# Moving matmul operands to fixed offsets within 256 bytes of an SBUF partition

## The chip, the core and the metric

The kernel runs on one core of a Trainium2 chip. The metric is the device time of one execution in microseconds (us). The engines have these names in the profile: PE is TensorE's matmul, PEld its weight load, DVE is VectorE, ACT is ScalarE, POOL is GpSimd, SP is SyncE, which here issues DMAs.

## The reference

256 tokens of 1024 features, float32, pass through five layers in a row. Each one normalises, multiplies by weight matrices and adds its result to the residual `x`.

```
x = x + mixer(rmsnorm(x))            # gated delta rule and mLSTM over w_in (1024 x 5648), then w_out
x = x + w2(silu(w1 h) * w3 h)        # hidden size 2816
x = rmsnorm(x + gate(h) * ple)       # per-layer embedding
x = x + gate * rglru(h);  x = x + gate * peer_ffn(h)     # peer: 16384 experts, u and v of 1024 each
x = x + gate * fox_attention(h);  x = x + gate * peer_ffn(h)
```

In `peer_ffn` every token picks 128 of 16384 experts. The kernel computes all experts with dense matmuls and weights them by a matrix that holds zeros for the experts not picked.

## The kernel before, in words

**Split precision.** Every large product is taken in three terms. A float32 weight tile of 128 x 1024 arrives by DMA as `raw`. ACT writes its rounded copy `whi` (type float32r, line 209), and DVE or POOL writes the rest, `wlo = raw - whi` (lines 257 and 259). The activations have the same two parts, in tiles with an h and an l: `hh`/`hl` for the normalised input, `fh`/`fl` in the feed-forward layer, `oab` in the mixer, `xbh`/`xbl` in the recurrent layer, `p0`/`p1` for the embedding, and `rawh`/`rawl` for the input before its norm is known. The matmuls are high times high, high times low and low times high.

**Stream.** The class `Stream` hands out one weight tile after another in a fixed order, 766 in all, with four buffers of `raw` and two each of `whi` and `wlo`. SP's queue issues the loads. The order of all instructions is a planner's, at build time.

**Three loops use them.** `block` (matmul at line 323) makes one output of 128 features x 256 tokens from one weight tile: 24 matmuls, in which a 128 x 128 piece of the weights is loaded into the array and 256 columns of the activations are streamed through. `kblock` (line 1051) is the same with one activation tile and eight outputs. `tblock` (line 1065) turns it round: a 128 x 128 piece of `hh` or `hl` is loaded, and 512 columns of `whi` or `wlo` are streamed, 12 matmuls for one weight tile. Inputs of a norm with a shift are streamed with 258 columns.

**Stages by time.** Mixer to about 290 us; feed-forward to about 460 (22 hidden tiles, three weight tiles each); embedding and recurrent layer to about 660; first peer layer: queries and selection to 811, `u` (128 blocks of line 323) to 1126, `v` (120 of line 1065 and 8 of line 1051) to about 1480; attention to about 1660; second peer layer likewise, `u` from 1822 to 2136 and `v` from there to the end. During `u`, DVE also builds one-hot matrices (lines 1584 to 1591), from which small float16 matmuls (line 1600) make the weighting.

**Where the tiles stand.** Tiles follow each other in a partition by their sizes, behind 16384 bytes of DMA scratch and 128 of constants. So before the change `hh` starts 24704 bytes into each partition and `hl` 32896, both 128 bytes beyond a multiple of 256. The stream's buffers start at 44480 and all stand 192 beyond one. `oab`, `xbh`, `xbl`, `p0`, `p1` and the 256-wide `rawh` and `rawl` also stand 192 beyond, `fh` and `fl` 0. Every slice that a matmul takes of them is a multiple of 256 bytes long, so all slices of a tile stand alike. The 258-wide `rawh` and `rawl` are the exception: each of their eight rows is 1032 bytes long, and so stands 8 bytes further on than the row before it.

Of the kernel before, what the change touches and what calls it, by code (L numbers as in the profile page):

```python
# [8 lines left out]
F32 = mybir.dt.float32  # L9
FR = mybir.dt.float32r  # L10
# [7 lines left out]
P = 128  # L18
S = 256
D = 1024  # L20
KC = D // P
NFF = 22
NR = 11
EPS = 1e-6
BIG = 1e30
TB = 8
TAIL = 8
NLATE = 3
# [11 lines left out]
def _constants():  # L40
# [6 lines left out]
    z[C_IOTA] = c + 0 * r  # L47
    z[C_NGT] = np.where(c > r, -BIG, 0.0)
    z[C_NLT] = np.where(c < r, -BIG, 0.0)
    for i, b in enumerate(LBS):  # L50
# [131 lines left out]
class Stream:  # L182
# [16 lines left out]
    def _ahead(self, b, n, loads, his, los):  # L199
        while self.nl < min(n, loads) or self.nh < min(n, his) or self.ns < min(n, los):  # L200
            if self.nl < min(n, loads) and self.nl < self.ns + b.raw_bufs:
                t = b.spool.tile([P, D], F32, name="raw", tag="raw", bufs=b.raw_bufs)[:, :self.width(self.nl)]
                self.load = b.nc.sync.dma_start(t, self.seq[self.nl])
                self.raw[self.nl] = t
                self.nl += 1
                continue
            if self.nh < min(n, his) and self.nh < self.nl:
                t = b.spool.tile([P, D], FR, name="whi", tag="whi", bufs=b.hi_bufs)[:, :self.width(self.nh)]
                b.nc.scalar.copy(t, self.raw[self.nh])  # L209
                self.hi[self.nh] = t  # L210
                self.nh += 1
                continue
            if self.ns < self.nh:
                i = self.ns
                t = b.spool.tile([P, D], FR, name="wlo", tag="wlo", bufs=b.lo_bufs)[:, :self.width(i)]
                b.sub(t, self.raw.pop(i), self.hi[i].bitcast(F32), i)
                self.lo[i] = t
                self.ns += 1
                continue
            raise AssertionError  # L220
# [9 lines left out]
class Build:  # L230
# [29 lines left out]

    def mark(self, label):
        pass

    def ahead_of(self, gen, prio):

# [86 lines left out]
    def setup(self):  # L352
        nc, pp, d = self.nc, self.pp, self.d
        self.xT = pp.tile([P, KC, S], F32, name="xT")
        self.hh = pp.tile([P, KC, S], FR, name="hh")
        self.hl = pp.tile([P, KC, S], FR, name="hl")
        with self.tc.high_priority(offset=5000):
            for k in range(0, KC, 2):
                nc.sync.dma_start(self.xT[:, k:k + 2], d["xT"][:, k:k + 2])
        self.cst = pp.tile([P, N_PERSIST, P], F32, name="cst")  # L360
        self.cols = pp.tile([P, N_COLS], F32, name="cols")
        nc.scalar.dma_start(self.cols, d["cols"])
        nc.scalar.dma_start(self.cst, d["const"][:, :N_PERSIST])
        self.ident = self.cst[:, C_ID]
        self.ones = self.cst[:, C_ONE]
        self.mhalf = pp.tile([P, 1], F32, name="mhalf")
        nc.vector.memset(self.mhalf, -0.5)
        self.lam = self.colr("lam")
        self.mods = [pp.tile([P, 24], F32, name=f"mod{i}") for i in range(4)]
        self.gsc = [pp.tile([P, KC], F32, name=f"gsc{i}") for i in range(4)]  # L370

        order = []

        def add(k, lo=0, hi=None):
            n = d[k].shape[0]
            order.extend(d[k][i] for i in range(lo, n if hi is None else hi))

        add("w_in")
        add("w_ba")
        add("w_bb")  # L380
        add("w_out")
        for j in range(NFF):
            add("w1", j, j + 1)
            add("w3", j, j + 1)
            if j:
                add("w2", j - 1, j)
        add("w2", NFF - 1, NFF)
        add("w_ple")
        add("w_pg")
        for j in range(NR + GLAG):  # L390
            if j < NR:
                add("l_in", j, j + 1)
            if j >= GLAG:
                i = j - GLAG
                order.append(d["l_gate"][i][:, :2 * len(PAIRS[i]) * P])
        add("l_in", NR, 2 * NR)
        add("l_out")
        for l in (0, 1):
            if l:
                add("f_in")  # L400
                add("f_out")
            add(f"q{l}")
            add(f"u{l}")
            add(f"v{l}")
        self.ws = Stream(self, order)
# [83 lines left out]
                                            op0=OP.mult, op1=OP.subtract)  # L489

    def raw_tiles(self, pool, wide=True):
        w = S + 2 if wide else S
        return (pool.tile([P, KC, w], FR, name="rawh"), pool.tile([P, KC, w], FR, name="rawl"),
                pool.tile([P, S], F32, name="rawb"),
                lambda: (pool.tile([P, S], F32, name="rawt", bufs=2), pool.tile([P, 1], F32, name="rawc", bufs=2)))

# [78 lines left out]
    def mix(self, mp, scr):  # L575
        nc = self.nc
# [1 line left out]
        gab = mp.tile([P, 16, S], F32, name="gab")  # L578
        gz = mp.tile([P, H, S], F32, name="gz")
        mo = mp.tile([P, H, S], F32, name="mo")  # L580
        oab = mp.tile([P, 16, S], FR, name="oab")
        self.oab = [oab[:, 4 * i:4 * i + 4] for i in range(4)]
        self.norm(scr, self.colr("g_mix"), raw=(
            oab[:, 0:8], oab[:, 8:16], gab[:, 0], lambda: (gab[:, 1 + self.nraw % 2], None)))
# [57 lines left out]
        for src, o in ((self.oa, 0), (self.ob, 8)):  # L642
            for b in range(4):
                wh, wl = self.ws.get()
                for n in range(2):
# [7 lines left out]
                    else:  # L653
                        t = mp.tile([P, S], F32, name="mixt", bufs=2)
# [417 lines left out]
    def ffn(self, fp, scr, fin):  # L1072
        nc = self.nc
        self.sub_pattern = "D"
        self.phase("ffn")
        self.norm(scr, self.colr("g_ffn"), raw=self.raw_tiles(fp, False), paced=True)
        self.bg.append(self.mod_task)
        accs = [self.acc() for _ in range(4)]
        hm = {}
        for j in range(NFF + 1):  # L1080
            if j < NFF:
                p1 = self.linear(self.mmt())
                p3 = self.linear(self.aux("p3"))
                s = fp.tile([P, S], F32, name="fs", bufs=2)
                nc.scalar.activation(s, p1, AF.Silu)
                nc.vector.tensor_tensor(s, s, p3, op=OP.mult)
                h = fp.tile([P, S], FR, name="fh", bufs=3)
                l = fp.tile([P, S], FR, name="fl", bufs=3)
                self.split(h, l, s)
                hm[j] = (h, l)  # L1090
            if j:
                self.kblock(accs, *hm.pop(j - 1), j == 1, j == NFF)
            self.tick()
            if j == 8:
                pT = fin.tile([P, 2, S], F32, name="pT")
                nc.scalar.dma_start(pT, self.d["pT"])
                self.p_split = [fin.tile([P, 2, S], FR, name=f"p{i}") for i in range(2)]
                for k in range(2):
                    self.split(self.p_split[0][:, k], self.p_split[1][:, k], pT[:, k])
        for n in range(KC):  # L1100
            nc.vector.tensor_tensor(self.xT[:, n], self.xT[:, n], accs[n // 2][:, (n % 2) * S:(n % 2 + 1) * S],
                                    op=OP.add)
# [74 lines left out]
    def lru(self, fin, scr):  # L1177
        nc = self.nc
        with ExitStack() as es:
            lp = es.enter_context(self.tc.tile_pool(name="lru", bufs=1))  # L1180
            xb = lp.tile([P, NR, S], F32, name="xb")
            xh = lp.tile([P, NR, S], FR, name="xbh")
            xl = lp.tile([P, NR, S], FR, name="xbl")
            hs = lp.tile([P, NR, S], F32, name="hs")
            lam = self.lam
            self.phase("lru")
# [60 lines left out]
    def fox(self):  # L1247
# [3 lines left out]
        with ExitStack() as es:  # L1251
# [68 lines left out]
            def scores(h):  # L1320
# [5 lines left out]
                for i, (a, b, k) in enumerate(((0, P, mask[:, P:]), (P, 384, mask))):  # L1326
                    nc.vector.tensor_tensor_reduce(out=L[:, a:b], in0=ps[:, a:b], in1=k, scale=1.0, scalar=-BIG,
                                                   op0=OP.add, op1=OP.max, accum_out=m[:, i:i + 1])
# [95 lines left out]
    def peer(self, l):  # L1424
        nc = self.nc
# [3 lines left out]
        with ExitStack() as es:  # L1429
            gp = es.enter_context(self.tc.tile_pool(name="peer", bufs=1))  # L1430
            big = gp.tile([P, P, S], F32, name="big")
            flat = big.rearrange("p a b -> p (a b)")

            def region(kb, size):
# [3 lines left out]
            es1 = es.enter_context(ExitStack())  # L1438
            rp = es1.enter_context(self.tc.tile_pool(name="raw", bufs=1))
            self.phase(f"peer{l}")  # L1440
            self.norm(big[:, 112:128], self.gsc[mi], self.mods[mi][:, 0:8], raw=(
                rp.tile([P, KC, S + 2], FR, name="rawh"), rp.tile([P, KC, S + 2], FR, name="rawl"), big[:, 0],
                lambda: (big[:, 1 + self.nraw % 2], flat[:, 3 * S + self.nraw:3 * S + self.nraw + 1])))
            qT = region(0, 4096).rearrange("p (a b) -> p a b", a=16)
            sk = region(16, 2048).rearrange("p (a b) -> p a b", a=16)
# [125 lines left out]
            def spread():  # L1571


                nonlocal held
                H = TB // 2
                iop = io[:, None].to_broadcast([P, H, P, 2])
# [3 lines left out]

                for t0 in range(0, S, TB):
                    tq = slice(t0, t0 + TB)
# [36 lines left out]
            for a in range(16):  # L1619
# [5 lines left out]
                if a % 4 == 3:  # L1625
                    for tb in range(2):
                        ps = self.aux("sc")
                        for i in range(4):
                            b = a - 3 + i
# [10 lines left out]
            for e in range(P):  # L1640
# [4 lines left out]
                if held:  # L1645
                    a = op.tile([P, S], F32, name="act", bufs=3)
# [46 lines left out]
            for e in range(P):  # L1693
# [6 lines left out]
                h, l_ = self.hh[:, e % 4], self.hl[:, e % 4]  # L1700
# [40 lines left out]
```

## Time and profile before

| what | value |
|---|---|
| time, median of 3 runs | 2492.12 us (2492.01 to 2500.49) |
| the profiled execution's own time | 2497.24 us |
| its span, first to last instruction | 2495.4 us |
| PE busy, of the span | 95% |
| DVE, ACT, POOL busy | 77%, 50%, 29% |
| matmuls, each with a weight load | 17450 |
| mean granted TensorE clock | 0.985 of full speed |

The span is the time in which instructions ran; 1.8 us of the execution's own time lie around it. Busy time of PE overstates it, since matmuls are pipelined and their ends are modelled: what counts is the distance from the start of one matmul to the start of the next. Where PE never waits, a stretch's length divided by its number of matmuls gives that distance, and so does the distance of the starts of two neighbouring rows of the timeline divided by the count in the first.

### The profile page before, as it was taken

How to read it: one execution, taken by the hardware profiler on the slowest of the kernel's cores; microseconds unless marked ns; L12 is line 12 of the kernel's file. 1: busy time of each engine (PE TensorE's matmuls, PEld its weight loads, DVE VectorE, ACT ScalarE, POOL GpSimd, SP SyncE). 2: the span in 40 equal slices, each digit the busy share in tenths (PEclk: the TensorE clock that was granted, in tenths of full speed). 3: DMA queues.
4: the chain of work that ended last, by engine and by line, in shares of the span. 5: the costliest groups of instructions: out<-in, count | busy, mean ns of one | idle time of the engine just before them, and what ended most of it. 6: DMA issues, size and time to landing. Idle time of an engine off the chain costs nothing. (4 is left out here: it accounts for less than half of the span.)

```text
span 2495.4 us, 44808 instructions
## 1 busy us (share of the span) xinstructions
PE 2380.4 (95%) x17450; PEld 2226.6 (89%) x17450; DVE 1923.4 (77%) x3481; ACT 1256.8 (50%) x2229; POOL 716.1 (29%) x361
## 2 busy tenths in 40 slices
PE   8989999987998999999999998899799999999999
PEld 8989999887998999997888898789799999888888
DVE  7585866889598999986666668878979998655555
ACT  7644544665553444445444556555344444444444
POOL 4635300355666323330000026246522222000000
PEclk9999999989998999999999999999899999999999
DMA  5475677434554555557777755555455555566654
GB/s 192 154 242 190 208 250 251 165 115 137 168 170 139 166 169 161 171 166 245 238 237 244 223 173 192 203 176 161 127 170 161 173 167 169 186 194 191 190 193 152
DMA packets 127252, 460.26 MB, mean 184 GB/s; under 512 B 14128, under 2 KB 14784, under 8 KB 126784
## 3 DMA queue, kind: packets, MB, share of 16 engines
q1 hardware_dynamic: 126000, 454.55, 56.2%
q8 instruction: 136, 2.23, 0.4%
q10 hardware_dynamic: 1040, 2.86, 0.3%
q14 instruction: 76, 0.62, 0.1%
HBM read 456.29 MB, written 1.05 MB: 183 GB/s over the span
## 5 line engine op out<-in xcount | busy, mean ns | idle before, releaser
L209 ACT CAST whi<-raw 128x1024 fp32r<-128x1024 f32 (+1 forms) x766 | 800.8, 1046 | 1000.5 <-PE acc L1065 325.9
L257 DVE TENSOR_TENSOR wlo<-raw,whi 128x1024 fp32r<-128x1024 f32 (+1 forms) x551 | 694.2, 1260 | 378.9 <-ACT whi L209 363.9
L259 POOL TENSOR_TENSOR wlo<-raw,whi 128x1024 fp32r<-128x1024 f32 (+2 forms) x215 | 566.7, 2641 | 754.0 <-ACT whi L209 440.4
L1065 PE MATMUL acc<-whi,hh 128*128 128x512 f32 x960 | 260.5, 392 | 2.6 <-ACT whi L209 1.1
L323 PE MATMUL mm<-hh,whi 128*128 128x256 f32 x1704 | 247.5, 286 | 15.7 <-ACT whi L209 6.6
L1065 PE MATMUL acc<-whi,hl 128*128 128x512 f32 x960 | 259.4, 391 | 0.0
L1065 PE MATMUL acc<-wlo,hh 128*128 128x512 f32 x960 | 259.1, 392 | 0.0
L323 PE MATMUL mm<-hh,wlo 128*128 128x256 f32 x1704 | 245.1, 286 | 13.6 <-DVE wlo L257 11.2
L323 PE MATMUL mm<-hl,whi 128*128 128x256 f32 x1704 | 246.1, 284 | 5.8 <-POOL hl L531 2.9
L323 PEld LDWEIGHTS mm<-hh,whi 128*128 128x128 f32 x1704 | 219.6, 191 | 20.1 <-ACT whi L209 7.8
L323 PEld LDWEIGHTS mm<-hh,wlo 128*128 128x128 f32 x1704 | 219.6, 192 | 16.2 <-DVE wlo L257 12.4
L323 PEld LDWEIGHTS mm<-hl,whi 128*128 128x128 f32 x1704 | 220.5, 192 | 8.3 <-POOL hl L531 4.0
L323 PE MATMUL acc<-hh,wlo 128*128 128x256 f32 x1464 | 207.6, 286 | 14.8 <-DVE wlo L257 12.0
L1065 PEld LDWEIGHTS acc<-whi,hh 128*128 128x128 f32 x960 | 180.1, 188 | 43.1 <-ACT whi L209 1.6
L1065 PEld LDWEIGHTS acc<-whi,hl 128*128 128x128 f32 x960 | 180.3, 188 | 39.8
L1065 PEld LDWEIGHTS acc<-wlo,hh 128*128 128x128 f32 x960 | 180.3, 188 | 39.3
L323 PE MATMUL acc<-hh,whi 128*128 128x256 f32 x1464 | 210.0, 286 | 0.1
L323 PE MATMUL acc<-hl,whi 128*128 128x256 f32 x1464 | 204.6, 281 | 0.0
L323 PEld LDWEIGHTS acc<-hh,wlo 128*128 128x128 f32 x1464 | 189.9, 194 | 15.8 <-DVE wlo L257 12.6
L323 PEld LDWEIGHTS acc<-hh,whi 128*128 128x128 f32 x1464 | 187.4, 192 | 0.3 <-ACT whi L209 0.3
L323 PEld LDWEIGHTS acc<-hl,whi 128*128 128x128 f32 x1464 | 186.4, 190 | 0.0
L422 DVE SCALAR_TENSOR_TENSOR modw<-modw,cb 128x1024 f32<-128x1024 f32 x96 | 130.7, 1366 | 21.5 <-DMA modw<-in_mod_dram 15.2
(523 smaller groups left out, 3304.1 us busy)
## 6 DMA issues: line engine op xcount, KB each, us to landing
raw<-in_u_dram SPq DMA_DIRECT2D x256, 512.0 KB, 3.7
raw<-in_v_dram SPq DMA_DIRECT2D x256, 512.0 KB, 4.1
modw<-in_mod_dram SPq DMA_DIRECT2D x96, 512.0 KB, 4.7
raw<-in_w_dram SPq DMA_DIRECT2D x66, 512.0 KB, 4.3
raw<-in_w_in_dram SPq DMA_DIRECT2D x45, 512.0 KB, 4.2
raw<-in_f_in_dram SPq DMA_DIRECT2D x33, 512.0 KB, 3.6
raw<-in_q_dram SPq DMA_DIRECT2D x32, 512.0 KB, 3.6
raw<-in_l_in_dram SPq DMA_DIRECT2D x22, 512.0 KB, 3.5
```

The costliest lines, as they stand in the source:

```text
L209: b.nc.scalar.copy(t, self.raw[self.nh])
L257: self.anchor = self.nc.vector.tensor_tensor(out, a, b, op=OP.subtract)
L259: self.nc.gpsimd.tensor_tensor(out, a, b, op=OP.subtract)
L323: self.last_mm = mm(ps, t[a], t[b], start=(i == 0), stop=(i == n - 1))
L422: self.later(nc.vector.scalar_tensor_tensor(t, t, 1.0, cb, op0=OP.mult, op1=OP.mult, accum_out=self.mods[i][:, j:j + 1]))
L1065: self.last_mm = mm(accs[h][tb], x[:, tb * P:(tb + 1) * P], w[:, h * 512:(h + 1) * 512], start=(first and i == 0), stop=(last and i == 2))
```

## The change

The computation, the instructions and their order in the source stay as they are; tiles get other places.

- `raw`, `whi` and `wlo` are allocated at multiples of 256 bytes.
- A new helper, `xtile`, allocates a tile at a multiple of 256 bytes with 32 unused elements (128 bytes) in front, and returns what follows them. `hh`, `hl`, `oab`, `rawh`, `rawl`, `fh`, `fl`, `p0`, `p1`, `xbh` and `xbl` are made by it.
- The 258-wide `rawh` and `rawl` get rows of 320 elements (1280 bytes, five times 256), of which 258 are used.
- The DMA scratch shrinks from 16384 bytes of a partition to 1024.

```diff
+ROW = 256
+HALF = 32
+RAWW = 320
...
-                t = b.spool.tile([P, D], F32, name="raw", tag="raw", bufs=b.raw_bufs)[:, :self.width(self.nl)]
+                t = b.spool.tile([P, D], F32, name="raw", tag="raw", align_bytes=ROW, bufs=b.raw_bufs)[:, :self.width(self.nl)]
...
-                t = b.spool.tile([P, D], FR, name="whi", tag="whi", bufs=b.hi_bufs)[:, :self.width(self.nh)]
+                t = b.spool.tile([P, D], FR, name="whi", tag="whi", align_bytes=ROW, bufs=b.hi_bufs)[:, :self.width(self.nh)]
...
-                t = b.spool.tile([P, D], FR, name="wlo", tag="wlo", bufs=b.lo_bufs)[:, :self.width(i)]
+                t = b.spool.tile([P, D], FR, name="wlo", tag="wlo", align_bytes=ROW, bufs=b.lo_bufs)[:, :self.width(i)]
...
+    def xtile(self, pool, n, name, w=S, **kw):
+        t = pool.tile([P, HALF + n * w], FR, name=name, align_bytes=ROW, **kw)
+        return t[:, HALF:].rearrange("p (a b) -> p a b", a=n)
...
-        self.hh = pp.tile([P, KC, S], FR, name="hh")
-        self.hl = pp.tile([P, KC, S], FR, name="hl")
+        self.hh = self.xtile(pp, KC, "hh")
+        self.hl = self.xtile(pp, KC, "hl")
...
-        w = S + 2 if wide else S
-        return (pool.tile([P, KC, w], FR, name="rawh"), pool.tile([P, KC, w], FR, name="rawl"),
+        w, n = (RAWW, S + 2) if wide else (S, S)
+        h, l = (self.xtile(pool, KC, k, w)[:, :, :n] for k in ("rawh", "rawl"))
+        return (h, l,
...
-        oab = mp.tile([P, 16, S], FR, name="oab")
+        oab = self.xtile(mp, 16, "oab")
...
-                h = fp.tile([P, S], FR, name="fh", bufs=3)
-                l = fp.tile([P, S], FR, name="fl", bufs=3)
+                h = self.xtile(fp, 1, "fh", bufs=3)[:, 0]
+                l = self.xtile(fp, 1, "fl", bufs=3)[:, 0]
...
-            xh = lp.tile([P, NR, S], FR, name="xbh")
-            xl = lp.tile([P, NR, S], FR, name="xbl")
+            xh = self.xtile(lp, NR, "xbh")
+            xl = self.xtile(lp, NR, "xbl")
...
-    nc = _bacc.Bacc("TRN2", target_bir_lowering=False, num_devices=1)
+    nc = _bacc.Bacc("TRN2", target_bir_lowering=False, num_devices=1, dynamic_dma_scratch_size=1024)
```

`p0`, `p1` and the peer layers' `rawh` and `rawl` change in the same way.

## Rows read from the trace of the kernel before

**Rows 1.** The page's busy times, and TensorE's granted clock in 40 slices.

```profile
PE 2380.4 (95%) x17450; PEld 2226.6 (89%) x17450; DVE 1923.4 (77%) x3481; ACT 1256.8 (50%) x2229; POOL 716.1 (29%) x361
...
PEclk9999999989998999999999999999899999999999
```

**Rows 2.** Chain of work that ended last, by line, shares of the span.

```profile
PE acc L1065 13%; PE mm L1051 0%; PE aux L1051 0%; DVE xT L1173 0%; PE back L1687 0%; ACT hh L340 0%; DVEq L1735 0%; ACT act L1647 0%
```

**Rows 3.** Stretches of PE: length, busy (matmuls), granted clock, DMA share, GB/s.

```profile
301.00:457.00 156.00, 156.00 (x1327) 1.00 0.73 245
...
1134.00:1430.00 296.00, 294.85 (x1288) 1.00 0.75 239
2140.00:2455.00 315.00, 315.00 (x1378) 1.00 0.61 191
...
0.00:300.00 300.00, 275.11 (x2208) 0.98 0.57 196
457.00:811.00 354.00, 310.46 (x2456) 0.94 0.44 145
1458.00:1822.00 364.00, 326.37 (x2578) 0.97 0.52 171
```

**Rows 4.** Timeline of PE, first peer layer's u: start us, us, instructions, count.

```profile
823.00 1.10 PE L323 MATMUL acc<-hh,whi 128*128 128x256 f32 x8
823.94 1.11 PE L323 MATMUL acc<-hl,whi 128*128 128x256 f32 x8
```

**Rows 5.** Timeline of PE, same stage, another three blocks.

```profile
1031.00 1.07 PE L323 MATMUL acc<-hh,wlo 128*128 128x256 f32 x8
1031.91 1.07 PE L323 MATMUL acc<-hh,whi 128*128 128x256 f32 x8
```

**Rows 6.** Timeline of PE, embedding layer, at the step from rawh to hh.

```profile
478.54 1.12 PE L323 MATMUL acc<-rawl,whi 128*128 128x256 f32 x8
479.50 1.12 PE L323 MATMUL acc<-rawh,wlo 128*128 128x256 f32 x8
...
482.29 1.07 PE L323 MATMUL mm<-hh,wlo 128*128 128x256 f32 x8
483.20 1.07 PE L323 MATMUL mm<-hh,whi 128*128 128x256 f32 x8
```

**Rows 7.** Timeline of PE, feed-forward layer, one kblock of fh and fl.

```profile
342.43 1.11 PE L1051 MATMUL acc<-fh,whi 128*128 128x256 f32 x8
343.37 1.10 PE L1051 MATMUL acc<-fl,whi 128*128 128x256 f32 x8
```

**Rows 8.** Timeline of PE, first peer layer's v (tblock).

```profile
1202.09 1.08 PE L1065 MATMUL acc<-wlo,hh 128*128 128x512 f32 x4
1203.01 1.08 PE L1065 MATMUL acc<-whi,hh 128*128 128x512 f32 x4
```

**Rows 9.** Timeline of PE, recurrent layer, 258-wide rows.

```profile
513.21 1.13 PE L323 MATMUL acc<-rawh,whi 128*128 128x258 f32 x8
514.18 1.12 PE L323 MATMUL acc<-rawl,whi 128*128 128x258 f32 x8
515.14 1.12 PE L323 MATMUL acc<-rawh,wlo 128*128 128x258 f32 x8
```

**Rows 10.** Two stretches of u: length, busy (instructions) of PE, PEld, DVE, ACT, POOL.

```profile
812.00:1097.00 285.00, 283.81 (x2633) 281.48 (x2632) 280.30 (x417) 125.75 (x270) 94.95 (x30) 1.00 0.52 166
...
1822.00:2106.00 284.00, 284.00 (x2644) 282.66 (x2642) 267.91 (x419) 125.24 (x270) 74.12 (x31) 1.00 0.53 167
```

**Rows 11.** DVE's line 1585 in u of both peer layers: busy us, mean ns.

```profile
L1585 DVE TENSOR_TENSOR ohB<-ohB,items 128x1024 bf16<-128x1024 bf16 x30 | 73.5, 2450 | 0.0
...
L1585 DVE TENSOR_TENSOR ohB<-ohB,items 128x1024 bf16<-128x1024 bf16 x30 | 20.3, 677 | 0.0
```

**Rows 12.** DMA queues: kind, packets, MB, share of 16 engines.

```profile
q1 hardware_dynamic: 126000, 454.55, 56.2%
...
q10 hardware_dynamic: 1040, 2.86, 0.3%
```

More of the change, by code (lines that the diff above doesn't have):

```diff
@@ L1096, in ffn @@
                 nc.scalar.dma_start(pT, self.d["pT"])
-                self.p_split = [fin.tile([P, 2, S], FR, name=f"p{i}") for i in range(2)]
+                self.p_split = [self.xtile(fin, 2, f"p{i}") for i in range(2)]
                 for k in range(2):
@@ L1440, in peer @@
             self.phase(f"peer{l}")
+            rh, rl = (self.xtile(rp, KC, n, RAWW)[:, :, :S + 2] for n in ("rawh", "rawl"))
             self.norm(big[:, 112:128], self.gsc[mi], self.mods[mi][:, 0:8], raw=(
-                rp.tile([P, KC, S + 2], FR, name="rawh"), rp.tile([P, KC, S + 2], FR, name="rawl"), big[:, 0],
+                rh, rl, big[:, 0],
                 lambda: (big[:, 1 + self.nraw % 2], flat[:, 3 * S + self.nraw:3 * S + self.nraw + 1])))
```

## The prediction

> **What bounds the kernel now.** I read the page's busy times and slices first: PE is busy for 95% of the span, at the full clock but for a few slices [rows 1]. The chain of work that ended last is PE's alone in the last stage [rows 2]. Next I read stretches. In the feed-forward layer and in both v stages PE has work all the time, so there the distance between two matmul starts is the time [rows 3]: 156 us for 1327 matmuls is 117.6 ns for 256 columns; 315 us for 1378 is 228.6 ns for 512 columns. In both u stages PE is full too, but DVE is nearly so: 280.3 of 285 us in the first, 267.9 of 284 in the second [rows 10]. The other 1018 us, three stretches, hold waits: PE is busy for 275.1 + 310.5 + 326.4 = 912 of them [rows 3].
>
> The granted clock is 1.00 in the full stretches, which is the 2.4 GHz level; at one column in a clock 256 columns would take 106.7 ns and 512 would take 213.3. Each matmul takes 4 to 15 ns more than that, and the change can only act on this part. The timeline shows that it is not one constant:
> - `hh` with `whi`, the first peer layer: 0.94 us for eight, 117.7 ns each [rows 4].
> - The same tiles in the same stage, 200 us later: 0.905 us, 113.2 ns [rows 5].
> - `rawh` and `rawl`, 256 wide: 0.96 us, 120 ns; three us later `hh` at 113.2 ns, with the same shape, line and clock [rows 6].
> - `fh`: 0.94 us, 117.7 ns [rows 7].
> - tblock, 512 columns: 0.92 us for four, some 229 ns [rows 3, 8].
>
> Beside the tiles' places this gives a pattern. Call distance how far, modulo 256 bytes, the start of the streamed slice stands from the start of the loaded one. `rawh` has distance 0 and the slowest steps; `hh`, `fh` and tblock have 64 to one side or the other, and 117.7, at times 113.2. The change makes it 128 everywhere. For `block` with `hh` that moves only the weights, since `hh` stands 128 beyond a multiple of 256 already.
>
> **The change part by part.**
> 1. *No instruction is added or removed.* Some 15300 split-precision matmuls (counted from the code: 1584 in the feed-forward layer, 2 x 3072 in u, 2 x 1632 in v, 4290 in the rest) have new places; ACT's and DVE's casts and subtractions have the same lengths. Padding is never read.
> 2. *DMA scratch.* All traffic is on two queues of the hardware kind [rows 12], so nothing uses the scratch but as space: zero. It pays for the padding. Weight loads land at multiples of 256 bytes; the DMA engines are busy for at most 0.75 in the full stretches [rows 3] and PE does not wait for them there: zero, and if that cover went, the DMA share would have to pass 1, which a pace faster by a few per cent doesn't bring about.
> 3. *Waits.* Buffer counts are unchanged, so no wait is added. A faster PE would bring the wait for DVE's `wlo` forward in u, which is counted below.
> 4. *The pace of a matmul.* No row shows distance 128 alone. From above: 120 ns, the steps at distance 0 [rows 6]. From below: 106.7 and 213.3 ns, one column in a clock. The nearest rows disagree. The fastest steps that this trace has for 256 columns are 113.2 [rows 5, 6], from the same tiles that give 117.7 elsewhere; so the extra time depends on how loads and streams fall against each other, and distance 0 is the worst. But 258-wide `rawl` rows whose distances run from 96 to 152, with 128 among them, take 0.96 us for eight, hardly less than the 0.97 of `rawh` at 32 to 88: 120 ns, some 119 for 256 columns [rows 9]. Half of these start 8 bytes off a multiple of 16 and each stands otherwise than the next, so I give them less weight. I take 113.3, the best that placement gives today, hence 4.4 ns less for each full-pace matmul; for tblock the same 4.4 ns, as its load is the same 128 x 128.
>
> The sum, by stages:
> - Feed-forward: 22 x 72 = 1584 matmuls x 4.4 = 7.0 us.
> - u of the first peer layer: 3072 x 4.4 = 13.5, but DVE has 285 - 280.3 = 4.7 us to spare [rows 10]: 5. Part of DVE's time isn't its own work: line 1585 takes 2450 ns here and 677 in the other peer layer, with the same shape [rows 11], so this limit may shift by some us either way.
> - u of the second: 13.5 wanted, 284 - 267.9 = 16.1 spare [rows 10]: 10, as not all of the spare time lies where it is needed.
> - Both v: 240 x 12 = 2880 x 4.4 = 12.7 us; ACT, DVE and DMA have room.
> - The rest: of its 4290 matmuls 978 stand at distance 0 (`oab` 288, `xbh` and `xbl` 450, 256-wide `rawh` and `rawl` 192, `p0` and `p1` 48) and 384 are 258 wide; 978 x 6.7 and 384 x 7 are 9.2 us; about half of it is on the path, as PE waits in these stages anyhow: 5.
>
> Together 40 us. The profiled execution took 2497.2, 5 above the median, so it would take 2457; from the median, 2492 - 40 = 2452. I say 2453.
>
> **Rivals.**
>
> *Nothing happens (2491).* The extra 4 to 15 ns may belong to the change of weights as such, and 117.7 stay at distance 128, as rows 9 suggest. Then only the 978 at distance 0 gain 2.3 ns each, half of it on the path: 1 us. For it: rows 9, and that distances of 64 on either side give the same 117.7. Against it: the step in rows 6 comes with the place alone. The Trainium skill speaks for this rival: its page "SBUF — State Buffer", section "Who interferes with whom", gives TensorE two independent read ports, one for the moving operand and one for weight loads, and says that it never waits on anyone; by that rule no placement matters and the sum is zero. This trace doesn't agree as far as distance 0 goes (120 against 113.2 ns, rows 6).
>
> *Much more (2401).* All extra time is a clash of the two reads and goes at 128: 11.0 ns less for 256 columns, 15.3 for 512. Feed-forward 17.4; first u 5, where DVE is the bound; second u 16, likewise; v 2880 x 15.3 = 44; the rest 1362 x 13.4 / 2 = 9: 91 us. Part of the way: 256 more columns cost 228.6 - 117.7 = 110.9 ns, so a matmul that paid for columns alone would take 110.9 and 221.8, which saves 6.8 on each; feed-forward 10.8, u 5 and 16, v 19.6 and the rest 6 make 57 us, 2435. Against it: no stretch of the trace runs that fast. The Trainium skill would put the result here: "TensorE: Matmul & The Clock Gate", section "Back-to-back issue gap", gives N/2.4 + 2.5 ns for an isolated matmul, 109.2 and 215.8; an estimate with it is 13 + 5 + 16 + 37 + 8 = 79 us, 2413. The trace agrees with neither figure (117.7 and 228.6, rows 3).
>
> *Slower (2526).* The new distance holds every matmul at the slowest step, 120 ns: 2.3 ns more for 1584 + 6144 + 2880 of them, 24 us, and 6.7 more for the 2928 others that now reach 113.2, half on the path, 10. For it: today's distance has a fast mode [rows 5] that can be lost, and distance 0 shows that a fixed relation can be stuck at the worst. Against it: the worst was seen at distance 0, which the change removes. It decides from about 1 ns per matmul on, a step of 118.8, where the loss passes 0.5%.
>
> **How the numbers follow.** A measurement of this kernel can tell about 0.5%, 12 us, from no change. Forecast, the fast mode everywhere: 0.42, its own range 2435 to 2475. Much more: 0.18. Nothing: 0.26. Slower: 0.14. So faster 0.60, same 0.26, slower 0.14. The predicted time is that of the forecast, 2453. The range goes up through the case of nothing to 2502 and down to 2400, which leaves out most of the slower case and some of the much faster one, about 2 in 10.
>
> **What would show it.** In the timeline of the feed-forward and u stages eight matmuls of 256 columns should step by 0.90 to 0.91 us, not 0.94, and four of tblock by 0.90, not 0.917; `rawh` should step like `hh`. In the stretches, the second v should hold some 1405 matmuls in 315 us. In the first u DVE should come to 99% busy and PE begin to wait for `wlo`; if instead PE stays full at 113 ns, the time above 677 ns in line 1585 gave way. Steps of 0.94 and 0.917 would show the first rival, 0.96 the last; steps below 0.89 the second. The prediction is wrong above all if distance is not what matters, and, in size, if DVE in u takes less time once PE runs faster.

## The result and the profile after

The changed kernel takes 2517.22 us (median of 4 runs, 2514.35 to 2519.24), the kernel before 2492.49 us in the same comparison: a ratio of 1.0092, with a 95% interval of 1.0072 to 1.0112. It is slower by 0.9%, where a gain of 1.6% was forecast; the time lies above the stated range, near the rival that was called slower (2526).

First the page of the changed kernel, against [rows 1]: busy times, and the granted clock.

```profile
PE 2410.7 (96%) x17450; PEld 2248.5 (89%) x17450; DVE 1920.7 (76%) x3481; ACT 1257.2 (50%) x2229; POOL 707.4 (28%) x361
...
PEclk9999999989999999999999999999899999999999
```

The instruction counts are the same, and PE issues all 17450 matmuls in the same order. PE's busy time has grown by 30 us and PEld's by 22; that of the other engines has hardly changed, and the clock has not fallen. The stretches of PE say where. They answer to the first and third of [rows 3] (the second is taken 20 us later, as the stage begins some 15 us later).

```profile
301.00:457.00 156.00, 156.00 (x1317) 1.00 0.74 244
...
2160.00:2475.00 315.00, 315.00 (x1357) 1.00 0.61 189
```

In equal time PE makes fewer matmuls: 1317 for 1327 in the feed-forward layer, or 118.5 ns for 117.6; 1357 for 1378 in the second v, 232.1 ns for 228.6. With these lines (331, 1060 and 1074 are the former 323, 1051 and 1065), the timeline shows the steps. First the first peer layer's u, against [rows 4, 5]:

```profile
828.05 1.11 PE L331 MATMUL acc<-hh,whi 128*128 128x256 f32 x8
829.00 1.11 PE L331 MATMUL acc<-hl,whi 128*128 128x256 f32 x8
829.95 1.11 PE L331 MATMUL acc<-hh,wlo 128*128 128x256 f32 x8
...
1040.71 1.11 PE L331 MATMUL mm<-hh,whi 128*128 128x256 f32 x8
1041.66 1.11 PE L331 MATMUL mm<-hl,whi 128*128 128x256 f32 x8
```

Eight matmuls now step by 0.95 us in both places: 118.7 ns, where there were 117.7 and 113.2. Then the embedding layer, against [rows 6], and the 258-wide rows, against [rows 9]:

```profile
481.08 1.11 PE L331 MATMUL acc<-rawl,whi 128*128 128x256 f32 x8
482.04 1.11 PE L331 MATMUL acc<-rawh,wlo 128*128 128x256 f32 x8
482.98 1.12 PE L331 MATMUL mm<-hh,whi 128*128 128x256 f32 x8
483.94 1.11 PE L331 MATMUL mm<-hl,whi 128*128 128x256 f32 x8
...
515.73 1.14 PE L331 MATMUL acc<-rawh,whi 128*128 128x258 f32 x8
516.71 1.14 PE L331 MATMUL acc<-rawl,whi 128*128 128x258 f32 x8
```

The step from `rawh` to `hh` is gone: both take 0.94 to 0.96 us for eight. `rawh` gains a little against its 0.96; `hh` goes from its 0.905 to 0.95. The 258-wide rows got slower too, 0.98 us for 0.96 to 0.97.

The loss by stages, from the starts of the same matmul in both traces: 5.0 us at the first float16 matmul of the first u (809.7 before, 814.7 after), 5.8 at the first tblock (1126.8 and 1132.6), 15.4 at the last float16 matmul of the second u (2115.6 and 2131.0) and 20.5 at the last tblock (2465.0 and 2485.5). The two v stages account for 2880 x 3.5 ns = 10 us of this, the stages with 256 columns for the other half.

### The profile page after: what moved, and what is told of

It reads as the page before. It is cut to its first block, busy times and chain, and to the rows that moved or that the text cites. A ratio compares the mean times of both kernels' runs of the same rounds, so it can differ in the third digit from the quotient of the medians.

```text
span 2516.7 us, 44808 instructions
## 1 busy us (share of the span) xinstructions
PE 2410.7 (96%) x17450; PEld 2248.5 (89%) x17450; DVE 1920.7 (76%) x3481; ACT 1257.2 (50%) x2229; POOL 707.4 (28%) x361
```

## The experiments

Each is told against the kernel before, which ran beside it on the same chip; ratios are with 95% intervals. My theory after the result: the step is set by the distance between the streamed and the loaded slice, modulo 256 bytes, and 128 is just not a good one. Its rivals: the smaller scratch or the padding cost the time; the weights' own place matters, not its distance from the activations; places don't matter at all.

**1. The small scratch alone.**

```diff
 # the kernel before
-    nc = _bacc.Bacc("TRN2", target_bir_lowering=False, num_devices=1)
+    nc = _bacc.Bacc("TRN2", target_bir_lowering=False, num_devices=1, dynamic_dma_scratch_size=1024)
```

> The kernel before with one part of the change alone, the small DMA scratch. All tiles move down by 15360 bytes, 60 times 256, so every place modulo 256 stays. Theory (the distance between the streamed and the loaded slice sets the step): 2492 us, ratio 1.000, eight matmuls of hh and whi step by 0.94 us in the feed-forward layer and four of tblock by 0.917. Rival (the smaller scratch or the lower addresses cost the time): about 2515 us, ratio 1.009.

Measured: 2497.41 us, ratio 1.0007 (0.9997 to 1.0017). The scratch costs nothing clear of noise, at most some 4 us.

The total came as expected, but not the step in the feed-forward layer: the profile holds 1359 matmuls in 156 us, where the kernel before has 1327 [rows 3]. `fh` and `fl`, at distance 64, keep 0.94 us for eight. `hh` and `hl`, at distance 192, take 0.91 through the whole layer:

```profile
301.00:457.00 156.00, 156.00 (x1359) 1.00 0.76 249
```

```profile
341.61 1.10 PE L1051 MATMUL acc<-fh,whi 128*128 128x256 f32 x8
342.55 1.10 PE L1051 MATMUL acc<-fl,whi 128*128 128x256 f32 x8
...
346.25 1.07 PE L323 MATMUL mm<-hh,wlo 128*128 128x256 f32 x8
347.16 1.07 PE L323 MATMUL p<-hh,whi 128*128 128x256 f32 x8
```

All tiles stand as before, modulo 256, so one distance can give two steps in two executions. Runs 5 to 7 come back to this.

**2. The weights back at 192, all else as changed.**

```diff
-                t = b.spool.tile([P, D], FR, name="whi", tag="whi", align_bytes=ROW, bufs=b.hi_bufs)[:, :self.width(self.nh)]
+                t = b.spool.tile([P, D + 64], FR, name="whi", tag="whi", align_bytes=ROW, bufs=b.hi_bufs)[:, 48:48 + self.width(self.nh)]
 # wlo likewise
```

> The changed kernel with whi and wlo 192 bytes beyond a multiple of 256, as they stood before; the activations stay 128 beyond one, padding and small scratch stay. Theory: the steps of hh with whi return to 117.7 ns and at times 113.3, tblock's to 229; oab, xbh and the 256-wide rawh come from 120 to the same steps; so the time is 2485 to 2492 us, ratio to the kernel before 0.997 to 1.000. Rival (padding, wider rows or the scratch cost the time, not the place of the weights): it stays near 2515, ratio 1.009.

Measured: 2495.09 us, ratio 0.9993 (0.9982 to 1.0003). The loss is gone with the weights' place alone; what padding, wide rows and the activations at 128 do together stays within the interval. The stretches of PE show the old steps, 117.6 and 228.6 ns:

```profile
301.00:457.00 156.00, 156.00 (x1327) 1.00 0.75 245
2160.00:2440.00 280.00, 280.00 (x1225) 1.00 0.62 192
```

**3 and 4. A sweep over 16 places in one run, with the activations at 128 and at 0.**

```diff
 # whi (index self.nh) and wlo (index i) of the changed kernel; in run 4 also HALF = 0
-  t = b.spool.tile([P, D], FR, ...)[:, :self.width(i)]
+  o = 4 * (i % 16)
+  t = b.spool.tile([P, D + 64], FR, ...)[:, o:o + self.width(i)]
```

> The changed kernel with whi and wlo of weight tile i standing 16 x (i mod 16) bytes beyond a multiple of 256; the activations stay 128 beyond one. So every stage goes through 16 places. Theory (distance modulo 256 alone): for 256 columns the step is a function of the place: 120 ns at 128 (distance 0), 117.7 or 113.3 at 192, 118.6 at 0; for tblock 229 at 192 and 232.4 at 0. Rival 1 (the place of the weights alone, wherever the activations stand): the same here, told apart by the next run. Rival 2 (places don't matter, the trace's history does): no dependence, 117 to 119 at all 16.

> As the sweep before it, but the activations stand at multiples of 256, without the 128 bytes in front. Theory (distance modulo 256 alone): the curve of the step over the weights' place is moved by 128 bytes against the sweep before: 120 ns at 0, 118.6 at 128, and at 64 what 192 gave. Rival 1 (the place of the weights alone): the same curve over the weights' place as in the sweep before. Rival 2: no dependence.

Measured: 2510.78 and 2517.64 us, one run each. The mean distance of two matmul starts in ns, at full clock, where the next matmul has the same places, without waits (steps of 150 ns and more are left out for 256 columns, of 270 and more for 512). Distance is the streamed start minus the loaded one, modulo 256 bytes; for 512 columns the weights are what streams.

```
distance    0     16    32    48    64    80    96    112   128   144   160   176   192   208   224   240
256, run 3  119.6 118.8 116.8 116.8 117.3 118.1 119.7 119.2 119.1 119.8 118.3 118.8 114.4 119.1 118.4 118.3
256, run 4  119.6 118.6 116.7 116.8 117.4 118.1 119.7 119.1 118.9 119.8 117.8 118.8 114.1 117.9 118.3 118.4
512, run 3  230.2 231.3 233.4 232.8 229.9 230.6 234.2 231.2 233.0 232.2 233.3 230.9 233.3 234.7 232.5 227.5
512, run 4  230.1 231.3 233.6 232.8 229.9 230.5 234.3 231.2 232.9 232.2 233.3 230.9 233.2 234.5 232.4 227.8
```

As functions of the distance the two runs agree within 0.3 ns at 30 of 32 places, though each place of the weights means another distance in the second: the curve has moved by 128 bytes with the activations. So it is the relation of the two slices that counts, not the weights' own place, and it counts to 5 ns and more. The timeline shows it for weights at 128 in run 3, then at 0 and, behind the dots, at 64 in run 4:

```profile
885.89 1.12 PE L333 MATMUL mm<-hh,whi 128*128 128x256 f32 x8
886.85 1.12 PE L333 MATMUL mm<-hl,whi 128*128 128x256 f32 x8
```

```profile
813.77 1.12 PE L333 MATMUL mm<-hl,whi 128*128 128x256 f32 x8
814.73 1.12 PE L333 MATMUL mm<-hh,wlo 128*128 128x256 f32 x8
...
876.46 1.07 PE L333 MATMUL acc<-hh,whi 128*128 128x256 f32 x8
877.37 1.07 PE L333 MATMUL acc<-hl,whi 128*128 128x256 f32 x8
```

Distance 0 gives 0.96 us for eight with either place of the activations, distance 192 gives 0.91. Best for 256 columns is 192, the one that `hh` had before the change; for 512 columns it is 240, and next comes 64, the one that tblock had. At 128 both are near the slow end, 119 and 233. Rival 1 falls, and so does rival 2 in that places do matter. In both sweeps each tile follows one that stands 16 bytes lower, so the table has each distance as it is entered from one neighbour alone.

**5 to 7. Better places than before the change?** All have the activations at 128. In 5 the v stages' weights stand at 112 (distance 240), the rest at 192; 6 and 7 also move `wlo` outside the v stages, to 176 and to 80.

```diff
 # vset: indices of the 120 tblock tiles of each v stage; LO is 48 in run 5, 44 in run 6, 20 in run 7
+  o = 28 if self.nh in b.vset else 48        # whi
+  o = 28 if i in b.vset else LO              # wlo
```

> As the run with weights at 192, but in the two v stages whi and wlo of the tblocks stand 112 bytes beyond a multiple of 256, 16 before the activations (streamed minus loaded: 240, where the sweeps had their fastest 512-column steps). Theory (the distance sets the step, whatever came before): four tblock matmuls step by 0.910 us (227.5 ns each), not 0.917; 2880 x 1.5 to 2.3 ns = 4 to 7 us less, ratio to the kernel before 0.997 to 0.998. Rival (the sweep's step came from changing places at every weight tile): the v stages stay at 229 ns or more and the ratio at 1.000.

> As the run before it, and in all other stages whi at 192 and wlo at 176, so that each block leaves distance 192 for eight matmuls and comes back. Theory (at distance 192 two modes are possible, and which one holds is set by what ran just before; a step from 208 to 192 sets the fast one, as in the sweeps): in the feed-forward layer eight whi matmuls step by 0.91 us and eight wlo ones by 0.94 to 0.95, a mean of 115.3 ns where 117.7 stood: 3.8 us there, some 7 to 15 in both u, with the v stages 15 to 25 in all, ratio 0.990 to 0.994. Rival (the mode is set by the stage's load, and dense stages run at 117.7): whi keeps 0.94, wlo gets 0.95, and the ratio is 1.000 or above.

> As the run before it, but wlo at 80 instead of 176 (distance 48, 116.8 ns in the sweeps, against 119.1). Theory: if a step from 48 to 192 sets the fast mode too, whi steps by 0.91 us and wlo by 0.935, a mean of 114.5 ns: some 3 us better than the run before it. If it doesn't, whi keeps 0.94 and the mean is 117.4, about 1 us better than weights at 192 alone, plus what the v stages gain. Rival as before: whi keeps 0.94 whatever the step.

Measured: 1.0064 (1.0043 to 1.0084), 1.0085 (1.0066 to 1.0105) and 1.0021 (1.0000 to 1.0042). All three miss, because of the v stages. The stretches of PE in run 7 are of the feed-forward layer and the two v stages:

```profile
301.00:457.00 156.00, 156.00 (x1364) 1.00 0.76 249
1150.00:1430.00 280.00, 280.00 (x1237) 1.00 0.74 239
2160.00:2440.00 280.00, 280.00 (x1185) 1.00 0.60 186
```

With the same places, the first v stage runs at 280 / 1237 = 226.4 ns and the second at 236.3. Within these stretches the step doesn't change. It does change early in the first v, across the one wait that PE has there: for ACT's `whi`, behind the fourth weight tile. In run 5 four matmuls step by 0.91 us ahead of that wait and by 0.95 behind it, to the end of the stage:

```profile
1134.44 1.07 PE L1079 MATMUL acc<-whi,hl 128*128 128x512 f32 x4
1135.35 1.07 PE L1079 MATMUL acc<-wlo,hh 128*128 128x512 f32 x4
1137.15 1.19 PE L1079 MATMUL acc<-whi,hh 128*128 128x512 f32 x4 [0.73 <-ACT whi L213]
1138.18 1.11 PE L1079 MATMUL acc<-whi,hl 128*128 128x512 f32 x4
1139.13 1.11 PE L1079 MATMUL acc<-wlo,hh 128*128 128x512 f32 x4
```

In run 7 the same wait lies between steps of 0.935 and 0.907 us. The second v has no wait behind its first weight tile, and keeps its step from there on.

A slow stage costs 1440 x 10 ns = 14 us, and run 7's twelve times fall into three groups, as if none, one or both of the v stages were slow: 2479.8; four from 2492.9 to 2497.7; seven from 2503.6 to 2509.0. The profiled execution, with one slow stage, is in the second group (2494.0). So neither my theory for run 5 nor its rival held: the sweep's step is real, but there is a second, slower one at the same distance. In the profiles of runs 5 and 6 both v stages were slow.

The 256-column stages have two modes as well. In run 5, whose feed-forward layer stands as in run 2, it ran at 113.4 ns (1376 matmuls) and not at 117.6. The second line is run 5's second v, a slow one:

```profile
301.00:457.00 156.00, 156.00 (x1376) 1.00 0.77 254
2160.00:2440.00 280.00, 280.00 (x1185) 1.00 0.61 185
```

In the feed-forward layer runs 6 and 7 came near what was hoped: with `wlo` at another distance for eight matmuls of each block, the layer's mean was 116.0 (1345 matmuls) and 114.4. That is below run 2's 117.6 but not below run 5's 113.4, so a single profile of this layer shows no gain. The u stages show one. By the starts of their 256-column matmuls, waits left out, both u run at 115.5 to 115.6 ns in the profiles of runs 7, 8 and 10, and at 117.6 to 117.8 in those of the kernel before and of runs 1, 2 and 5.

**8. The same without the v stages' risk**, and **9. the change with the v stages alone undone.**

```diff
 # run 8: as run 7, but the v stages' weights at 192
-  o = 28 if i in b.vset else 20
+  o = 48 if i in b.vset else 20
 # run 9: the change, but the v stages' weights at 192
+  o = 48 if i in b.vset else 0
```

> The run with whi at 192 and wlo at 80, but with the v stages' weights back at 192 (distance 64, where no run has shown a slow mode). Theory (at some distances a stage can fall into one of two steps and keep it; 64 for 512 columns has one): the v stages step at 229 ns in every execution, the feed-forward layer and both u keep the mean of about 114.5 they had in that run, 11 us less than before the change in its profile up to the second v; so 2480 to 2486 us, ratio 0.994 to 0.997, and the spread between executions shrinks. Rival (the gain up to there was one execution's luck): ratio 1.000.

> The changed kernel with one part undone: the v stages' weights stand at 192 again, all others stay at multiples of 256. Theory: tblock returns from 232.4 to 229 ns, 2880 x 3.4 = 10 us of the change's 21 come back, ratio to the kernel before 1.004 to 1.006, and the other stages keep 118.6 ns. Rival (the v stages' loss comes from what stands around them, such as the rows of hh and hl or the padding): 232.4 stays, ratio 1.009.

Measured: run 8 takes 2485.78 us (2484.14 to 2488.53), ratio 0.9968 (0.9958 to 0.9978). It beats both kernels, if by 0.3%, and its nine times span 4.4 us where fourteen of the kernel before span 9.3 beside it. Its stretches of PE:

```profile
301.00:457.00 156.00, 156.00 (x1365) 1.00 0.76 251
1150.00:1430.00 280.00, 280.00 (x1224) 1.00 0.71 237
2160.00:2440.00 280.00, 280.00 (x1225) 1.00 0.63 192
```

The feed-forward layer has 114.3 ns, both v stages 228.6 to 228.8. Run 9 has 1.0046 (1.0030 to 1.0062): the v stages are half of the loss, the 256-column steps the other half. In its stretches the feed-forward layer stays as slow as with the change, and the second v is back at 228.6 ns:

```profile
301.00:457.00 156.00, 156.00 (x1317) 1.00 0.73 242
2160.00:2440.00 280.00, 280.00 (x1225) 1.00 0.64 192
```

**10. Can the entry pick the mode?** As run 7, with the first two tiles of each v stage at 96 (vin).

```diff
+  o = 24 if i in b.vin else 28 if i in b.vset else 20
```

> As the run with whi at 192, wlo at 80 and the v stages' weights at 112, but the first two weight tiles of each v stage stand at 96 (distance 224), from which the sweep went to distance 240 and its 227.5 ns nearly every time. Theory (what runs just before sets the step, and a stage that isn't interrupted keeps it): both v stages step at 227.4 ns in nearly all executions, 2880 x 1.6 = 5 us better than with the weights at 192 there: some 2481 us, ratio 0.994 to 0.996. Rival (the slow step of 236.6 sets in later, by chance, whatever the entry): times spread as in that run, between 2480 and 2509, ratio 0.999 to 1.004.

Measured: 0.9996 (0.9984 to 1.0007), 2488.84 to 2504.60. In its profile the first v is slow (280 / 1185 = 236.3) and the second fast (226.4), the reverse of run 7:

```profile
1150.00:1430.00 280.00, 280.00 (x1185) 1.00 0.71 231
2160.00:2440.00 280.00, 280.00 (x1237) 1.00 0.64 194
```

Eleven of twelve times lie from 2488.8 to 2496.5, where one slow stage of two would put them, and none at 2480. Run 7 had four of its twelve in the middle group, on another chip. That the two tiles changed the odds is likely, but not shown. The theory's figure was missed. The ratio is the rival's (0.999 to 1.004), with a narrower spread than it said.

The trace shows why the theory could fail in one stage and hold in the other. In the first v the wait behind the fourth weight tile comes after the two entry tiles. Ahead of it four matmuls at distance 240 step by 0.935 us, behind it by 0.95, to the end:

```profile
1129.62 1.09 PE L1080 MATMUL acc<-whi,hl 128*128 128x512 f32 x4
1130.55 1.10 PE L1080 MATMUL acc<-wlo,hh 128*128 128x512 f32 x4
1132.64 1.20 PE L1080 MATMUL acc<-whi,hh 128*128 128x512 f32 x4 [0.99 <-ACT whi L213]
1133.68 1.11 PE L1080 MATMUL acc<-whi,hl 128*128 128x512 f32 x4
1134.63 1.11 PE L1080 MATMUL acc<-wlo,hh 128*128 128x512 f32 x4
```

In the second v no wait follows the entry tiles; it goes from them to 0.907 us and stays there, as the theory says. That the entry decides where no wait follows is not shown by this one profile. Entry tiles behind the wait would test it.

## Why the prediction was wrong

**The step that failed** is the fourth of the part by part working, the pace: "I take 113.3, the best that placement gives today". At distance 128 the steps are 118.7 for 256 columns and 232.1 to 232.4 for 512. Instead of 4.4 ns less, the dense 256-column matmuls pay 1 ns more, those that reached the fast mode 5 ns more, and tblock 3.5 ns more. Two choices led there. From steps of 120 at distance 0 and 113 to 118 at 64 on either side I gave 128 the best step of all, as if the step fell with the distance; the sweep shows a curve with several dips, the deepest of them at the place left, and distance 0 is not the one worst: 96 and 144 equal it for 256 columns, and for 512 it is among the better. And rows 9, the only ones with 128 among their distances, said 119 for 256 columns; I had them on the page and gave them less weight for their 8-byte steps. They came within half a ns of the 118.7, in part by luck: 258-wide rows that all stand at 128 take 0.98 us for eight in the changed kernel, 122 ns where those mixed rows had 120.

**The bounds.** 120 held from above for 256 columns. For tblock no bound above was given, and I moved it by the same 4.4 ns as the others; it went the other way, and by more than the slower rival's 2.3.

**The sum's other terms** had no occasion to be tested by the change, as PE became slower: DVE remains below its limit in both u (279.0 of 285 us and 266.5 of 284). Run 8 bears on the terms of u, where it has 115.5 ns for 117.6: the first u holds 2650 matmuls in 285 us for 2633 [rows 10], 0.6% more, and the second 2687 in 284 for 2644, 1.6%. In the first, PE waits 2.6 us for POOL's `wlo` (1.1 before); in the second it waits for nothing. No wait of PE in these stretches is put down to DVE, which the prediction took for the bound.

**What was right.** Scratch and padding cost nothing clear of noise (runs 1 and 2). Placement does change the step, so the rival of no effect was wrong: the two sweeps move the step by 5 ns with nothing but places. The Trainium skill's page "SBUF — State Buffer", section "Who interferes with whom", had spoken for that rival, with two independent read ports and a TensorE that never waits on anyone. The conclusion drawn from it, that no placement matters, doesn't hold here; whether the two reads hold each other up, no run shows. The slower rival had the right sign and in part the right reason, a fast mode lost where `hh` had it; its price of 34 us was some 10 too high (24.7 between the medians), since 128 holds the steps at 118.7, not 120, and tblock's 3.5 ns made up only a part. I gave it 0.14.

**What stays open.** Whether overlapping loads and streams clash, which of them, and why in this pattern of distances, wasn't measured. The sweeps had the activations at 128 and at 0; for other places of theirs only 192 is known, at distance 0 (120 ns, [rows 6]). Nor is it known what picks one of the steps at 192 and at 240. In the v stages of runs 5, 7 and 10 it changed across a wait of PE, but which step follows a wait, the runs don't tell.

## What to carry to other kernels

Where matmuls run back to back, count them in a stretch: a step that differs between tiles of the same shape and clock can be a matter of where the operands stand. One run with places that change from tile to tile measures the curve, though not a second step at the same place. A place can have two steps, so judge it by many executions of the whole kernel, and prefer one that has shown no slow step. When a row of the trace comes near the new state, however untidy, it deserves at least the weight of a trend through two points.

## What the runs showed of the hardware

- The distance, modulo 256 bytes, between the starts of the streamed and the loaded slice changes the step of float32r matmuls at full clock: 114 to 120 ns for 256 columns, 227.5 to 234.7 for 512 (runs 3 and 4).
- At some distances there is more than one step: 113.4 or 117.6 ns at 192 with 256 columns (runs 5 and 2, and run 1 against the kernel before), 226.4 or 236.3 at 240 with 512 (runs 7 and 10). A v stage changed its step only early, across a wait of PE of about 1 us or behind its entry tiles, and kept it from there to the end. With 14 us for each v stage, this makes a spread between executions of one program.
- With `wlo` at distance 48 for eight matmuls out of 24 and `whi` at 192 for the others, both u run at 115.5 to 115.6 ns in three profiles of three, for 117.6 to 117.8 with all at 192 (runs 7, 8 and 10). With it run 8 gains 0.3%. Going to another distance is not enough by itself: in the feed-forward layer of the kernel before, `fh` and `fl` are at 64 between blocks at 192, and in its profile all stay at 117.6.
